# Batched gelu, a combination behind another tile, and the room of the transposed queries given to weight slots

## The chip, the cores and the metric

The kernel runs on one core of one Trainium2 chip. The metric is the time of one execution on the device in microseconds (us). A core has a matrix engine (TensorE, PE in the profile; PEld is its loading of weights), three engines for elementwise work (VectorE or DVE, ScalarE or ACT, GpSimd or POOL), and SyncE (SP), which here issues all DMA transfers. Each engine runs its own list of instructions in order and waits on semaphores for the others. TensorE writes to PSUM, eight banks per core; everything else lies in SBUF, 128 partitions wide, or in the chip's main memory.

## The reference, cut to what matters

Four residual layers over 1024 tokens of 1024 values: a mixer and a gated MLP, twice. The change lies in the first mixer alone, which projects the normalised tokens once and splits the columns: u and v (512 each) feed a gated branch, q, k and vb (512 each, eight heads of 64) feed attention in dilated windows. Both results side by side go through an output projection.

```python
u, v, q, k, vb = split(rms_norm(x, g) @ w_in)

# gated branch: chunks of 128 tokens, 8 channel groups
vn = layer_norm(gelu(v), ln_g, ln_b)
mixed = einsum('gts,bnsgc->bntgc', tril(w_s), vn) + b_s
a_out = gelu(u) * mixed

# attention: three branches, windows 128, 512, 2048, strides 1, 4, 16
qh, kh = rms_norm(heads(q), q_g), rms_norm(heads(k), k_g)
for window, dilation in ((128, 1), (512, 4), (2048, 16)):
    o, lse = dilated_branch(qh, kh, vh, window, dilation)   # softmax inside the window
b_out = sum of the branches' o, weighted by softmax of their lse

x = x + concat(a_out, b_out) @ w_out
```

Then follow the first MLP, a chunked gated linear attention, and the second MLP. All is float32 to the reader; the kernel splits an operand of a large matmul into a rounded part and a remainder (`split`, `scaled`, lines 98 to 106: the rounded part on ScalarE, the remainder on VectorE) and runs three matmuls for one product (`PASSES`).

## The kernel before

The text of the kernel is a program in one thread. A planner in the compiler lays it out when the kernel is built: it simulates the engines and writes each engine's list, where earlier text goes first among what is ready, and it adds the semaphores. `tc.keep_in_program_order(ins)` ties an instruction behind the one that the text has just before it on the same engine. A tile pool hands out room: a tag with `bufs=n` has n places in turn, and a new tile waits until the readers of the one n before it are done. Pools opened with `side="right"` lie at the other end of SBUF.

`even` (line 509) is the first mixer. The tokens come in eight tiles of 128. They are transposed and split into `hq`, and the row norms are kept in `r0`. Then come four pairs of heads (`project`, line 676, and `dilated`, line 737), the gated branch (`gmlp`, line 574; `u_proj`, line 612), and, in `out_first` (line 432), the output projection.

- `project(p)` needs eight weight pieces (`load_qkv`, line 564; tile names wq). Each is loaded raw (pool `rawp`, four places), scaled and split into one of the eight places of `wp`. The next pair's pieces, the eight of v (wv), of u (wu) and of the output projection (wo) use the same eight places one after the other. For each token tile it projects into PSUM (pj, two places), normalises queries and keys (lines 693 to 699), transposes them, and copies the queries to qT (line 713), from there to qR in the order of the strided branch (line 715, POOL), and the keys to kT. `unit` (line 650) does the attention of one token tile: scores (line 641), mask and maximum (646), exponential (647), transposes (661), product with the values (669). qT, qR and kT are as long as all tokens; pairs 0 and 2 have theirs in pool `pq0` on the right side, pairs 1 and 3 in `pq`. `par0.close()` gives the right side back behind pair 3's projection, and the gated branch's pool `gm` takes it.
- `dilated(p)` does the strided branches from qR, kT and v4 and stores the result (od). It comes back from memory as on, and `combine` and `combined` (lines 754 to 779) weigh both with an exponential (763), a few small VectorE instructions and one product on POOL and one on VectorE (776), add them (778) and store the pair's columns to `bcat` (779), one tensor per half of the tokens. For pairs 0 to 2 this runs inside the next pair's projection, behind its token tiles 3 and 4. For pair 3 it is `last` (line 804).
- `gmlp` projects v tile by tile (pv, in pj's PSUM places). `consume` (589) takes each tile through gelu, mean and variance, normalisation, gain and bias into mx; behind the last tile of each half of the tokens come eight group matmuls (pm, 605) and the additions of b_s (606).
- `u_proj` projects u (pu), takes each tile through gelu (616) and multiplies it into mx (617). Behind its fifth tile it calls `last`. The first instruction of a combination on VectorE (759) is pinned by `keep_in_program_order`.
- `out_first` loads each tile's part of bcat (cat, line 1122), transposes mx and cat (pc, 442), splits them into hq, and multiplies by wo (po, line 190 by the helper `mm_tok`).

## Time and profile before

| | us |
|---|---|
| median of 3 runs | 2196.88 (2193.66 to 2197.9) |
| the profiled execution's own time | 2195.83 |
| its span, first to last instruction | 2194.0 |
| TensorE busy | 2147.0 |
| VectorE busy | 1533.2 |
| ScalarE busy | 1042.7 |
| TensorE busy in 262 to 272 (pair 3, v) | 9.71 of 10 |
| in 272 to 332 (v, pair 3's attention) | 58.20 of 60 |
| in 332 to 394 (u) | 58.94 of 62 |
| in 394 to 405 | 1.50 of 11 |
| in 405 to 480 (output projection, first half) | 75.00 of 75 |

A line of a timeline has the start in us from the span's start, the duration, the engine, the line of the kernel, the operation, output<-inputs with the tiles' names, the shape, how many were merged, and in brackets the idle time of the engine before it with what ended it. A line of waits has who waited, for whom, the total, how many times, and the longest. A line of windows has the stretch, its length, then busy time and number of instructions of each engine, the clock granted to TensorE (1.00 is full), the share of time that the DMA engines were busy, and GB/s. A group of instructions has the line, engine, operation, tiles, shape and count, then busy us and mean ns of one, then the engine's idle time before them. An ACT_TABLE_LOAD is ScalarE exchanging its function tables, which stands under the line of the activation that needs it. Matmul ends are modelled and overlap, so a busy TensorE isn't one at its peak.

### The profile page before, as it was taken

Reading aid. Unit: us, or ns where it says so; the run is one execution under the profiler, and the core shown is the slowest. Engines: PE = TensorE matmul, PEld = TensorE weight load, DVE = VectorE, ACT = ScalarE, POOL = GpSimd, SP = SyncE. Lnnn points to the kernel's source line nnn. Section 1 sums busy time; section 2 is a strip of 40 time slices with the busy share of each in tenths; the row PEclk is TensorE's granted clock in tenths of the full one; section 3 lists DMA queues with packets and bytes.
Section 4 is the critical chain, followed back from the end, with each engine's and each line's share of the span. In section 5 each row is a group of like instructions: output and inputs, shape, how many; then the busy total and the mean of one; then the engine's idle time right before and its main releaser. Section 6 shows DMA issues by size and latency. Waiting matters only on the chain.

```text
span 2194.0 us, 29873 instructions
## 1 busy us (share of the span) xinstructions
PE 2147.0 (98%) x10508; PEld 1816.2 (83%) x10508; DVE 1533.2 (70%) x2459; ACT 1042.7 (48%) x2006; POOL 489.0 (22%) x519
## 2 busy tenths in 40 slices
PE   8999999899999999999999999999999999999999
PEld 8999987687888888878889788878788888888887
DVE  5566653567888788855577777667787878885554
ACT  6555664245444444444454455534544444454443
POOL 4444410003334342200010011110232424320000
PEclk9999999899999999999999999999999999999999
DMA  4122212565544444585563123377544454457555
GB/s 148 47 72 81 78 35 59 179 247 189 163 158 158 154 154 159 187 291 179 204 236 113 68 97 104 104 258 265 194 145 153 158 165 157 168 176 268 204 195 203
DMA packets 157254, 349.59 MB, mean 159 GB/s; under 512 B 17408, under 2 KB 54272, under 8 KB 156720
## 3 DMA queue, kind: packets, MB, share of 16 engines
q1 hardware_dynamic: 157104, 347.68, 46.9%
q8 instruction: 83, 1.36, 0.3%
q14 instruction: 67, 0.55, 0.1%
HBM read 239.02 MB, written 108.59 MB: 158 GB/s over the span
## 4 chain that ended last, share of the span: by engine, by line
PE 88%; DVE 4%; DMA 3%; ACT 3%; issue 1%; POOL 1%; SPq 0%; ACTq 0%; DVEq 0%
PE puB L290 11%; PE pgB L290 11%; PE po L190 7%; PE pj L190 6%; PE pgC L290 5%; PE puC L290 5%; PE pv L190 5%; PE pdB L397 5%; PE pdC L397 5%; PE pdO L397 4%; PE puA L290 3%; PE pgA L290 2%; PE pdP L397 2%; PE pdQ L397 2%; PE pBq L972 2%; PE pu L190 2%
## 5 line engine op out<-in xcount | busy, mean ns | idle before, releaser
L101 DVE TENSOR_TENSOR da<-ar,da 128x512 fp32r<-128x512 f32 x154 | 106.3, 690 | 156.2 <-ACT da L100 156.0
L100 ACT CAST da<-ar 128x512 fp32r<-128x512 f32 x154 | 95.9, 623 | 209.4 <-PE pdC L397 90.7
L190 PE MATMUL po<-wo,hq 128*128 128x512 f32 x768 | 186.4, 397 | 0.6 <-DVE hq L101 0.3
L190 PEld LDWEIGHTS po<-wo,hq 128*128 128x128 f32 x768 | 142.5, 189 | 30.2 <-DVE hq L101 1.4
L190 PE MATMUL pj<-wq,hq 128*128 128x384 f32 x768 | 157.8, 352 | 2.3 <-ACT vN L701 1.3
L190 PE MATMUL pv<-wv,hq 128*128 128x512 f32 (+2 forms) x768 | 141.1, 340 | 2.4 <-DVE b L1004 1.6
L190 PEld LDWEIGHTS pj<-wq,hq 128*128 128x128 f32 x768 | 135.3, 195 | 4.0 <-ACT vN L701 2.1
L397 PE MATMUL pdB<-dw,da 128*128 128x512 f32 x528 | 136.2, 391 | 0.9 <-ACT dw L100 0.9
L397 PE MATMUL pdC<-dw,da 128*128 128x512 f32 x528 | 135.8, 390 | 0.0
L190 PEld LDWEIGHTS pv<-wv,hq 128*128 128x128 f32 x768 | 118.7, 189 | 17.6 <-DVE b L1004 2.1
L397 PEld LDWEIGHTS pdB<-dw,da 128*128 128x128 f32 x528 | 98.7, 188 | 22.2 <-ACT dw L100 1.3
L397 PEld LDWEIGHTS pdC<-dw,da 128*128 128x128 f32 x528 | 99.0, 188 | 20.5
L256 POOL TENSOR_TENSOR S1g<-rg 128x512 f32<-128x512 f32 x20 | 29.3, 1464 | 384.2 <-DMA wsd<-D 325.0
L101 DVE TENSOR_TENSOR dw<-wr,dw 128x512 fp32r<-128x512 f32 x154 | 105.8, 687 | 10.7 <-ACT dw L100 10.4
L140 POOL TENSOR_SCALAR rn<-ssq 128x1 f32<-128x1 f32 x24 | 9.5, 397 | 461.3 <-ACT h L148 245.3
L397 PE MATMUL pdO<-dw,da 128*128 128x512 f32 x396 | 102.2, 389 | 0.2 <-DVE dw L101 0.2
L100 ACT CAST dw<-wr 128x512 fp32r<-128x512 f32 x154 | 95.0, 617 | 15.3 <-DMA wr<-in_w_dn 7.0
L397 PEld LDWEIGHTS pdO<-dw,da 128*128 128x128 f32 x396 | 74.3, 188 | 16.0 <-DVE dw L101 0.6
L319 DVE SCALAR_TENSOR_TENSOR t<-g,cw,t 128x1022 f32<-128x1022 f32 x44 | 75.6, 1719 | 0.1
L318 DVE SCALAR_TENSOR_TENSOR t<-g,cw,t 128x1023 f32<-128x1023 f32 x44 | 58.3, 1325 | 16.4 <-ACT t L317 16.4
L303 DVE TENSOR_TENSOR g<-g,s1g 128x512 f32<-128x512 f32 x22 | 16.2, 737 | 73.9 <-ACT s1g L302 73.9
L320 ACT ACTIVATE t<-t 128x1024 f32<-128x1024 f32 x44 | 46.7, 1061 | 29.8 <-DVE t L319 29.6
(1070 smaller groups left out, 5405.9 us busy)
## 6 DMA issues: line engine op xcount, KB each, us to landing
ar<-actd SPq DMA_DIRECT2D x70, 512.0 KB, 3.5
rd<-in_w_down SPq DMA_DIRECT2D x44, 512.0 KB, 3.6
wsd<-D SPq DMA_DIRECT2D x88, 256.0 KB, 2.6
rg<-in_w_gate SPq DMA_DIRECT2D x42, 512.0 KB, 3.6
ru<-in_w_up SPq DMA_DIRECT2D x42, 512.0 KB, 4.6
wr<-wsd SPq DMA_DIRECT2D x40, 512.0 KB, 4.5
actd<-t SPq DMA_DIRECT2D x66, 256.0 KB, 2.1
wr<-in_w_dn SPq DMA_DIRECT2D x30, 512.0 KB, 5.0
```

What stands on the lines that cost most here:

```text
L100: (hi or A.copy)(dst[0], src)
L101: (lo or V.tensor_sub)(dst[1], src, f32(dst[0]))
L140: G.tensor_scalar(r, ssq, 1.0 / n, EPS, op0=ALU.mult, op1=ALU.add)
L190: T.matmul(o, L[i], R[jj][:, sl], start=(k == 0 and (ii, jj) == PASSES[0]), stop=(k == nk - 1 and (ii, jj) == PASSES[-1]))
L256: G.tensor_tensor(sums[name], x, y, op=op)
L290: T.matmul(o, L[ii][:, j * P : j * P + P], right[p][:, jj, j, :], skip_group_check=more, start=(not more and j == 0 and (ii, jj) == PASSES ...
L303: V.tensor_add(C22, C22, s1)
L318: V.scalar_tensor_tensor(t[:, 1:], g[:, : S - 1], w(1), t[:, 1:], op0=ALU.mult, op1=ALU.add)
L319: V.scalar_tensor_tensor(t[:, 2:], g[:, : S - 2], w(0), t[:, 2:], op0=ALU.mult, op1=ALU.add)
L320: A.activation(t, t, AF.Silu)
L397: T.matmul(o, L[ii][:, t * P : t * P + P], R[jj], skip_group_check=more, start=start and not more and (ii, jj) == PASSES[0], stop=stop and ...
L972: T.matmul(o, L[ii][:, j * P : j * P + P], right[p][:, jj, j, :], skip_group_check=more, start=(not more and j == 0 and (ii, jj) == PASSES ...
```

## The change

Four things in `even`'s functions, none in what is computed.

- v's tiles are scaled by their row norm while they are copied from PSUM to mx. Behind the fourth tile of a half one gelu runs over all four (128x2048, in place), then the four normalisations and the group matmuls. The second half's gelu is pinned behind the copy before it. The tag gv goes, and u's tiles get their own tag ut with five places in place of gv's two.
- `last` is called behind u's second tile in place of its fifth.
- qT is a tile of one token tile (128x2x128), with three places in `pq` for all pairs, in place of one tile for all tokens in `pq0` and one in `pq`.
- A pool `wx` on the right side, opened ahead of `pq0` and closed with it, has four places of 128x2x384. The first four of the eight weight pieces of pairs 0 and 2 are split into it; the other four, and all of pairs 1 and 3, go to `wp` as before.

```diff
+            wx = par0.enter_context(tc.tile_pool(name="wx", bufs=4, side="right", reuse_waits="tile"))
             pq0 = par0.enter_context(tc.tile_pool(name="pq0", bufs=1, side="right", reuse_waits="tile"))
...
-    def load_qkv(p):
-        return [w for kp in range(4)
-                for w in load_w(a["w_qkv"][p, kp], f"wq{p}{kp}", 384, gains=g0[:, 2 * kp : 2 * kp + 2])]
+    def load_qkv(p, wx):
+        ws = []
+        for kp in range(4):
+            raw = load_raw(a["w_qkv"][p, kp], f"wq{p}{kp}r", 768)
+            for i in range(2):
+                k = 2 * kp + i
+                src, gain = raw[:, i * 384 : i * 384 + 384], g0[:, k : k + 1]
+                if p % 2 or k >= 4:
+                    ws.append(parts_of(src, f"wq{p}{kp}_{i}", gain=gain))
+                else:
+                    w = wx.tile([P, 2, 384], F32R, tag="wx", name=f"wx{p}{k}")
+                    ws.append([w[:, j, :] for j in range(2)])
+                    scaled(ws[-1], src, gain)
+        return ws
...
         def consume(n, pj):
-            gv = gm.tile([P, 512], F32, tag="gv", bufs=2, name=f"gv{n}")
-            A.activation(gv, pj, AF.Gelu, scale=r0[:, n : n + 1])
...
-            r = inv_rms(mv[:, 1:2], 1, 1, f"lr{n}")
-            V.tensor_scalar(gv, gv, mv[:, 0:1], r, op0=ALU.subtract, op1=ALU.mult)
-            V.tensor_mul(gv, gv, lnG)
             half, j = n // 4, n % 4
-            V.tensor_add(mx[half][:, j, :], gv, lnB)
-            if j == 3:
-                for g in range(GROUPS):
...
+            A.activation(mx[half][:, j, :], pj, AF.Copy, scale=r0[:, n : n + 1])
+            if j < 3:
+                return
+            ge = A.activation(flat(mx[half]), flat(mx[half]), AF.Gelu)
+            if half:
+                tc.keep_in_program_order(ge)
+            for j in range(4):
+                gv = mx[half][:, j, :]
...
+                r = inv_rms(mv[:, 1:2], 1, 1, f"lr{half}{j}")
+                V.tensor_scalar(gv, gv, mv[:, 0:1], r, op0=ALU.subtract, op1=ALU.mult)
+                V.tensor_mul(gv, gv, lnG)
+                V.tensor_add(gv, gv, lnB)
+            for g in range(GROUPS):
...
         def consume(n, pj):
-            t = gm.tile([P, 512], F32, tag="gv", bufs=2, name=f"ut{n}")
+            t = gm.tile([P, 512], F32, tag="ut", bufs=5, name=f"ut{n}")
             A.activation(t, pj, AF.Gelu, scale=r0[:, n : n + 1])
             V.tensor_mul(mixed[n], mixed[n], t)
-            if n == 4:
+            if n == 1:
                 last()
...
             pool = pq if p % 2 else pq0
-            qT = pool.tile([P, 2, S], F32R, tag="qT", bufs=1, name=f"qT{p}")
             qR = pool.tile([P, 2, S], F32R, tag="qR", bufs=1, name=f"qR{p}")
...
-                A.copy(qT[:, :, ts_], f32(tq))
+                qT = pq.tile([P, 2, P], F32R, tag="qT", bufs=3, name=f"qT{p}{n}")
+                A.copy(qT, f32(tq))
...
-                G.tensor_copy(four(qR), by4(f32(qT[:, :, ts_])))
+                G.tensor_copy(four(qR), by4(f32(qT)))
...
-                unit(p, f"{p}n{n}", n % 4, ot, po, lambda s: qT[:, s, ts_],
+                unit(p, f"{p}n{n}", n % 4, ot, po, lambda s, qT=qT: qT[:, s],
```

More of the change, by code (lines that the diff above doesn't have):

```diff
@@ L538, in even @@
                     tc.tile_pool(name="av", bufs=1, reuse_waits="tile") as av:
-                return attention(ps, at, av, pq, pq0, par0, wq0, masks, gm_open)
+                return attention(ps, at, av, pq, pq0, par0, wx, wq0, masks, gm_open)
     def band_masks(pool):
@@ L589, in consume @@
         def consume(n, pj):
[L590 to L606 removed]
+            half, j = n // 4, n % 4
+            A.activation(mx[half][:, j, :], pj, AF.Copy, scale=r0[:, n : n + 1])
[6 more added lines that the diff above has]
+                gv = mx[half][:, j, :]
+                st = small.tile([P, 6], F32, tag="bn", name=f"bn{half}{j}")
+                V.bn_stats(st, gv)
+                mv = small.tile([P, 2], F32, tag="mv", name=f"mv{half}{j}")
+                V.bn_aggr(mv, st)
+                r = inv_rms(mv[:, 1:2], 1, 1, f"lr{half}{j}")
[3 more added lines that the diff above has]
+            for g in range(GROUPS):
+                gc = mx[half][:, :, g * 64 : g * 64 + 64]
+                pm = ps.tile([P, 4, 64], F32, tag="sc", name=f"pm{half}{g}")
+                T.matmul(pm, ws[:, g, :], gc, start=True, stop=True)
+                V.tensor_scalar(gc, pm, bs[:, g : g + 1], None, op0=ALU.add)
         mx = [gm.tile([P, 4, 512], F32, name=f"mx{h}") for h in range(2)]
@@ L614, in consume, with attention @@
         def consume(n, pj):
[L615 removed]
+            t = gm.tile([P, 512], F32, tag="ut", bufs=5, name=f"ut{n}")
             A.activation(t, pj, AF.Gelu, scale=r0[:, n : n + 1])
             V.tensor_mul(mixed[n], mixed[n], t)
[L618 removed]
+            if n == 1:
                 last()
         proj512(ps, load_half(a["w_vu"][1], "wu", g0), "pu", consume)
[L623 removed]
+    def attention(ps, at, av, pq, pq0, par0, wx, wq0, masks, gm_open):
         gqk = pq.tile([P, 2, 2, 64], F32, name="gqk", bufs=1)
```

13 lines of the change are left out of this document (2 added, 11 removed).

## The prediction

> **What bounds the kernel now.** I read the page first (span, busy shares), then TensorE's waits in the first 420 us, where all changed code runs, then ten-microsecond windows with the granted clock, and last the order of time on each engine around the largest wait. All times below are those of the one profiled execution.
>
> ```profile
> span 2194.0 us, 29873 instructions
> PE 2147.0 (98%) x10508; PEld 1816.2 (83%) x10508; DVE 1533.2 (70%) x2459; ACT 1042.7 (48%) x2006; POOL 489.0 (22%) x519
> ```
>
> TensorE is busy for 98% of the span, so a change that removes none of its matmuls can only gain where it waits or where its clock is reduced.
>
> ```profile
> PE pc L442 <- DMA cat<-bcat: 9.3, 1, 9.3
> PE pP3d L661 <- ACT sm3d L647: 3.3, 3, 2.0
> PE po0n L669 <- DVE pT0n L666: 2.2, 2, 1.9
> PE pP1n L661 <- ACT sm1n L647: 1.4, 2, 1.0
> PE pj L190 <- ACT vN L701: 1.3, 3, 0.6
> PE pu L190 <- ACT ut L616: 0.9, 1, 0.9
> ```
>
> One wait is nearly three times the next: the transposes of the output projection (pc, line 442) stand 9.3 us for a load of bcat, the attention's combined heads. The next, 3.3 us, is a transpose that waits for the last pair's exponentials.
>
> ```profile
> core 0: us, PE busy (x) PEld busy (x) DVE busy (x) ACT busy (x) POOL busy (x), PEclk, DMA share, GB/s
> 60.00:70.00 10.00, 8.10 (x52) 7.87 (x51) 9.44 (x21) 6.14 (x15) 5.54 (x8) 0.92 0.39 107
> 70.00:80.00 10.00, 9.62 (x60) 9.41 (x59) 4.36 (x14) 4.85 (x14) 5.96 (x11) 0.91 0.22 68
> 140.00:150.00 10.00, 8.37 (x37) 7.70 (x38) 4.98 (x15) 4.51 (x14) 6.55 (x11) 0.68 0.32 102
> 330.00:340.00 10.00, 7.96 (x45) 6.90 (x44) 8.69 (x22) 9.94 (x20) 0.74 (x2) 0.91 0.60 184
> 360.00:370.00 10.00, 8.98 (x39) 6.76 (x38) 4.47 (x9) 1.29 (x2) 0.00 (x0) 1.00 0.34 83
> 403.40:406.00 2.60, 2.34 (x7) 1.60 (x8) 1.25 (x2) 1.07 (x2) 0.00 (x0) 0.50 1.03 387
> 406.00:409.00 3.00, 3.00 (x12) 2.60 (x12) 0.74 (x2) 0.59 (x1) 0.00 (x0) 0.50 1.00 405
> 409.00:412.00 3.00, 3.00 (x12) 2.40 (x12) 0.69 (x1) 0.59 (x1) 0.00 (x0) 0.87 0.44 125
> ```
>
> The column after POOL is the granted clock. It is 0.50 after the long wait, and 0.92, 0.91, 0.68 and 0.91 in the windows at 60, 70, 140 and 330 us, where TensorE also stood.
>
> ```profile
> 362.39 1.52 SPq L788 DMA_DIRECT2D on<-od  x2
> 367.42 1.29 DVE L617 TENSOR_TENSOR mx<-mx,ut 128x512 f32<-128x512 f32 x2
> 385.92 0.69 DVE L617 TENSOR_TENSOR mx<-mx,ut 128x512 f32<-128x512 f32 x1
> 386.53 0.16 DVE L759 TENSOR_TENSOR cM<-ot3n,on 128x8 f32<-128x8 f32 x1
> 393.23 0.36 SPq L779 DMA_DIRECT2D bcat<-ot3n  x1
> 397.82 0.47 SPq L1122 DMA_DIRECT2D cat<-bcat  x1
> 384.94 8.78 PE L190 MATMUL pu<-wu,hq 128*128 128x512 f32 x37
> 393.56 0.60 PE L442 MATMUL pc<-ident,mx 128*128 128x128 f32 x4
> 403.41 1.12 PE L442 MATMUL pc<-ident,cat 128*128 128x128 f32 x4 [9.25 <-DMA cat<-bcat]
> 404.77 1.22 PE L190 MATMUL po<-wo,hq 128*128 128x512 f32 x2 [0.25 <-ACT hq L100]
> ```
>
> This is why that load is late. The other operands of the last combination (on) were asked for at 362.39, but its first VectorE instruction (line 759) runs at 386.53, right behind the product of u's fifth tile (line 617, 385.92): program order pins it there, and that product needs the second half of the gated values. So the first half's store to bcat leaves at 393.23, the load that reads it at 397.82, and TensorE, through with u at 393.7, goes on at 403.41.
>
> **The change, part by part.**
>
> *Last combination behind u's second tile.* It removes and adds no instruction; twenty VectorE instructions, two exponentials, two products on POOL (idle in the row at 360) and two stores on SP move, the stores ahead of the loads of wo's second half. The new pin is the product of tile 1, which needs only the first half of the gated values. Both products of tiles 0 and 1 already ran from 367.42 on, and on was asked for at 362.39, so the combination can start near 368. Its load can follow 11.3 us later (386.53 to 397.82 now), near 380, and land after another 5.6 (397.82 to 403.41), near 386, against 394 when it is wanted: 8 us of cover. What is removed: the 9.25 us. What is late next: the output projection's weights. The last rounding of wo on ScalarE and its remainder on VectorE are these:
>
> ```profile
> 394.68 0.61 ACT L100 CAST wo<-wo03r 128x512 fp32r<-128x512 f32 x1
> 398.55 0.68 DVE L101 TENSOR_TENSOR wo<-wo03r,wo 128x512 fp32r<-128x512 f32 x1
> ```
>
> VectorE reaches the last remainder only at 398.55 because the combination's instructions from 386.53 on lie between the remainders. Without them it follows ScalarE's 394.68 + 0.61 and ends near 396.0. TensorE starts the first tile at 393.56 + 0.60 + 1.36 = 395.5 (the first transposes, then 403.41 to 404.77 as now) and needs this eighth piece last. So none of this wait stays; with VectorE as late as now (399.2) it would be at most 3.7 us. The clock: by the three rows from 403.40, 2.6 x 0.50 + 3.0 x 0.50 + 3.0 x 0.13 = 3.2 us were withheld, part of it while TensorE waited for hq (before 404.77); I take 2.5. The Trainium skill ("TensorE: Matmul & The Clock Gate", Part 1: The HAM clock gate) has half the clock after an idle window of about 3.4 us and until about 3.4 us of sustained work; by that the term would be 1.7 instead of 2.5, an estimate, and the sum 0.8 us smaller. The trace agrees on the half and shows it for at least 5.6 us.
>
> At its new place the combination shares VectorE (4.47 of 10 us busy at 360) and ScalarE (1.29) with little. Behind its first instruction, if on lands late, wait the additions of the second half's gated values (line 606) and, through their PSUM tiles, TensorE. on was asked for 5 us ahead of the products now; I charge 1.25 us for this and for two table loads between gelus, with 0 and 2.6 as bounds (two loads of the size below). Together: -9.25 - 2.5 + 1.25 = -10.5. Bounds: -9.25 - 3.2 = -12.5, and -9.25 + 3.7 + 2.6 = -3.0 if wo and the two loads are paid and the clock gives nothing.
>
> *Batched gelu.* Now each of v's eight tiles has its own gelu among the last pair's exponentials, and ScalarE exchanges its tables for each:
>
> ```profile
> L647 ACT ACT_TABLE_LOAD x9 | 11.5, 1283 | 12.1 <-DVE ot3d L646 6.5 <-DVE ot3n L646 5.5
> L591 ACT ACT_TABLE_LOAD x8 | 10.3, 1283 | 0.1
> L616 ACT ACT_TABLE_LOAD x3 | 3.8, 1283 | 0.3 <-PE pu L190 0.3
> 382.67 1.28 ACT L763 ACT_TABLE_LOAD   x1
> L148 ACT ACTIVATE n<-xt 128x1024 f32<-128x1024 f32 x8 | 8.6, 1074 | 16.9 <-DVE xt L429 15.8 <-ACT n L148 0.7 <-issue 0.5
> ```
>
> That is 21 loads of 1.283 us, 27 us. Two batches need two exchanges each, the combination two, u's first tiles some two: about 8, so 13 x 1.283 = 16.7 us go from ScalarE. Eight copies take the place of eight gelus on the same tiles, at about the same price; the two gelus of 128x2048 come on top, at twice the 1.07 us of the 128x1024 row, 4.3 in all. ScalarE gains 12 us, but it bounds nothing here: on TensorE only the waits behind it count, 3.3 + 0.9 of those quoted, and the clock at 330 (10 x 0.09 = 0.9), 5.1 together. Against it: one batch holds up every exponential behind it for 1.28 + 2.15 + 1.28 = 4.7 us, where now each gelu holds them up for half of that. TensorE has v's next tile to run meanwhile, since the copies empty its two PSUM tiles ahead of the gelu. VectorE gets a half's normalisation (four tiles of some 3 us) in one run, but it lies behind the attention in program order. ut gets five buffers in place of two, so the 0.9 us wait for ut goes. I take half: -2.5, with -5.1 and +4.7 (one batch uncovered) as bounds. The pin on the second batch names the copy just before it, on which it depends anyway; I give it nothing.
>
> *Four weight slots for even pairs.* Today the eight pieces of a pair are all split at the turn to the next pair, as slots come free:
>
> ```profile
> 60.00:70.00 10.00, 6.11 (x30) 5.45 (x29) 5.51 (x8) 4.44 (x8) 0.92 0.39 107
> 130.00:140.00 10.00, 8.07 (x44) 7.06 (x43) 6.12 (x8) 4.47 (x8) 1.00 0.48 126
> ```
>
> VectorE spends 5.51 and 6.12 of ten microseconds on them (the third busy time of a row, here of these splits alone), just where TensorE waits for pT0n (2.2 us) and sm1n (1.4). With the change pair 0 leaves four of the common slots free for pair 1, and pair 2 finds its own four free since pair 0; half of each burst, about 2.9 us of VectorE and 2.2 of ScalarE, moves ahead of the turn into windows where both have room. It adds no work; each split and its matmuls are as before. What is behind the bursts on TensorE: the waits 2.2 + 1.4 + 1.3, and the clock, 0.8 + 0.9 at 60 and 70 and 3.2 at 140: 9.8 us. The combinations stay at the turn, and four splits too, so I take two fifths: -4.0, with -9.8 as one bound. The other is +3: half a burst set in front of a row of exponentials elsewhere.
>
> *Queries per token tile.* Same copies (line 713) and readers; three tiles of room in place of eight. A tile's scores must be through before the copy three tiles on:
>
> ```profile
> 272.36 0.36 ACT L713 CAST qT<-tq 128x256 fp32r<-128x256 f32 x1
> 287.26 0.37 ACT L713 CAST qT<-tq 128x256 fp32r<-128x256 f32 x1
> 277.88 0.64 PE L641 MATMUL sc3n<-kT,qT 128*128 128x256 f32 x4
> 298.70 0.72 PE L641 MATMUL sc3n<-kT,qT 128*128 128x256 f32 x4
> ```
>
> In the last pair a copy's scores follow 5.5 us (272.36 to 277.88) to 11.4 us (287.26 to 298.70) behind it, and two copies further on lie 14.9 us: a ring of three isn't full. Zero, with 0 and the rival below as bounds.
>
> Sum: -10.5 - 2.5 - 4.0 + 0 = -17.0. The profiled execution took 2195.83 us (1.83 around its span of 2194.0) and the median of the three runs is 2196.88, 1.05 more. So 2195.83 - 17.0 + 1.05 = 2179.9; I say 2180. All that lies behind moves up with it, since TensorE is busy for 98% of the span.
>
> **Rivals.**
>
> *The ring of three becomes the wait: slower.* If each of the 32 tiles' copies waits for scores, ScalarE stands, and behind it exponentials and the emptying of pj. It decides from 17.0 / 32 = 0.53 us per tile; at 0.8 us the time is 2197 - 17 + 26 = 2206. For it: the planner's new order isn't known, and scores of a tile come up to 11.4 us late. Against: 14.9 us between copies.
>
> *Batches hold up the attention.* Both batches uncovered cost 9.4 us in place of the gain of 2.5: 2180 + 11.9 = 2192, or 2187 to 2189 with one and some of the weights' gain lost as well. For it: the wait for sm3d is of this kind already.
>
> *The load stays late or another takes its place.* If SP or VectorE puts the combination behind other work again, the largest term fails and 2197 - 6.5 = 2190 is left. Against: its pin, and 8 us of cover.
>
> *Nothing moves.* The batch loses what the slots gain, and the cat wait turns into one for wo and the DMA engines, which are busy to 1.03 and 1.00 at 403 and 406: 2197.
>
> *The clock doesn't come back.* Behind u TensorE has only transposes and a short wait. If transposes don't hold the clock, the output projection starts at 0.50 as now: 2180 + 2.5 = 2182.5. In the trace 140 us is such a stretch, mostly attention, at 0.68. The Trainium skill ("TensorE: Matmul & The Clock Gate", Part 4: PE-mode transpose) says that a transpose doesn't count as busy for the gate; the low clock at 140 agrees, but other waits stand there too. The stretch is about 2 us, so I give it little.
>
> **How the numbers follow.** Forecast 0.45; clock 0.12; batches 0.17; load late 0.10; nothing moves 0.05; slower 0.11. Faster by over 0.2% (4.4 us, about what a measurement of this kernel can tell from no change): 0.84; same 0.05; slower 0.11. The range runs from 2170, where the slots give 9.8 and the gelu 5.1 with some new wait against them, to 2193, which takes in the batches and the late load; what is left out is nothing moved, slower, and a little below: 0.2. The forecast's own range is 2172 to 2186.
>
> **What would show it.** Right: no wait of pc for cat; the combination's line 759 on u's pair near or before 370; clock near 1.00 right behind u; table loads in the first 420 us of about 8 in place of 21; fewer splits of wq in the windows of the turns, and waits there under 3 us. Wrong: a new wait of over 3 us at pP3d or pm behind the 128x2048 gelu, waits of ScalarE in front of qT, or the projection po waiting for wo.

## The result and the profile after

The changed kernel takes 2184.73 us (median of five runs, 2180.52 to 2186.67); the kernel before, on the same chip, 2197.45 (2193.66 to 2201.47). The ratio is 0.9943, with a 95% interval of 0.9925 to 0.9961: 12.7 us faster, where 17.0 were forecast. The profiled execution took 2186.67, 1.7 around its span. On the page:

```profile
span 2185.0 us, 29867 instructions
PE 2145.9 (98%) x10508; PEld 1817.9 (83%) x10508; DVE 1538.2 (70%) x2459; ACT 1032.7 (47%) x1998; POOL 488.4 (22%) x519
```

TensorE's busy time hardly moved (2147.0 to 2145.9); what went is waiting. From its list of waits in the first 420 us (waiter, whom for, total, times, longest):

```profile
PE pt L530 <- DMA x<-in_x: 5.5, 2, 4.4
PE tk L736 <- ACT qT L731: 1.7, 3, 0.6
PE pc L442 <- DVE hq L101: 1.7, 1, 1.7
```

The 9.3 for cat and the 3.3 for sm3d are gone. What is late next is small: pc for hq, 1.7, and the queries' copy, 1.7 in three parts. The timelines of VectorE, SyncE and TensorE show the combination in its new place:

```profile
366.30 1.29 DVE L635 TENSOR_TENSOR mx<-mx,ut 128x512 f32<-128x512 f32 x2
367.51 0.16 DVE L777 TENSOR_TENSOR cM<-ot3n,on 128x8 f32<-128x8 f32 x1
374.69 0.96 SPq L797 DMA_DIRECT2D bcat<-ot3n  x2
377.04 0.33 SPq L1140 DMA_DIRECT2D cat<-bcat  x1
387.08 0.44 PE L442 MATMUL pc<-ident,mx 128*128 128x128 f32 x2 [0.67 <-DVE mx L624]
387.36 0.38 PE L442 MATMUL pc<-ident,cat 128*128 128x128 f32 x2
388.41 0.73 PE L190 MATMUL po<-wo,hq 128*128 128x512 f32 x2 [0.24 <-ACT hq L100]
```

It starts right behind the first products, at 367.51 (386.53 before), its load leaves at 377.04 (397.82 before), and TensorE transposes cat at 387.36 with no wait. ScalarE's table loads and the batched gelu, in the groups of the stretch from 262 to 420:

```profile
L665 ACT ACT_TABLE_LOAD x4 | 5.1, 1283 | 0.1
L634 ACT ACT_TABLE_LOAD x4 | 5.1, 1283 | 0.1
L607 ACT ACTIVATE mx<-mx 128x2048 f32<-128x2048 f32 x2 | 3.8, 1918 | 0.0
L607 ACT ACT_TABLE_LOAD x2 | 2.6, 1283 | 0.0
L781 ACT ACT_TABLE_LOAD x1 | 1.3, 1283 | 0.0
```

Eleven loads in place of 21 (I had said about 8: u's tiles still fall among the last exponentials, with four loads).

**Where the time went.** The span is cut at TensorE's first or last matmul on a tile, read from its timeline: the end of pair 0's values (po0n), the start and end of v (pv), the end of u (pu), the first po, the first matmul of the MLP (pgB), the end of the span. Durations in us, of one profiled execution each; the experiments of the next section stand below the line of the changed kernel.

| kernel | to po0n's end | to v | v | u | to po | output proj. | rest |
|---|---|---|---|---|---|---|---|
| before | 91.14 | 180.76 | 59.98 | 61.84 | 11.05 | 102.28 | 1686.95 |
| changed | 95.80 | 176.84 | 55.21 | 58.13 | 2.43 | 106.16 | 1690.43 |
| changed, again | 95.92 | 176.83 | 55.18 | 58.13 | 2.43 | 106.09 | 1686.82 |
| 1: combination | 91.98 | 177.42 | 59.97 | 60.77 | 1.77 | 101.52 | 1689.87 |
| 2: gelu | 90.79 | 177.22 | 55.16 | 60.18 | 11.09 | 101.52 | 1689.14 |
| 3: slots and ring | 93.68 | 178.03 | 60.02 | 62.17 | 12.18 | 104.61 | 1690.61 |
| 3, again | 98.50 | 176.80 | 60.05 | 61.96 | 11.53 | 103.25 | 1690.61 |
| 4: changed, two places for u | 92.28 | 176.93 | 55.18 | 60.20 | 1.78 | 101.50 | 1691.03 |
| 5: gelu + combination | 90.69 | 180.39 | 55.17 | 60.21 | 1.77 | 100.28 | 1687.59 |
| 5, again | 91.61 | 178.96 | 55.17 | 60.21 | 1.77 | 100.28 | 1686.90 |
| 6: slots for pair 2 | 92.09 | 176.98 | 55.17 | 60.21 | 1.77 | 101.55 | 1690.83 |
| 7: 5 + 6 KB unused | 89.83 | 177.42 | 55.17 | 60.20 | 1.78 | 106.24 | 1687.16 |
| 8: 5 + five places, other room | 92.22 | 180.35 | 55.17 | 58.13 | 2.44 | 102.40 | 1689.29 |
| 9: ring | 92.14 | 179.12 | 61.13 | 60.75 | 10.99 | 103.54 | 1688.53 |

The changed kernel gains 4.8 in v, 3.7 in u and 8.6 ahead of po, and 3.9 up to v, but loses 4.7 in pair 0 and 3.9 in the output projection. In the rest, where no text was changed, two executions of one kernel differ by 3.6 (1690.43 and 1686.82; 1.7 of it is a stretch at half clock at 1445 us that only the first has), so nothing is read from that column, nor from a difference of 3 us between two spans.

The first two columns differ mostly by the clock. Take off the time that it withheld ahead of v (half the length of each stretch at half clock: 5.1 us before and in both executions of the changed kernel, 0 to 8.5 in the others). Then v's first matmul comes at 266.1 to 267.7 us in the eight executions without the four weight slots, and at 266.8 to 268.3 in the six with them. Up to there the slots neither gain nor lose anything that can be told apart from the clock.

Two things in the changed kernel weren't forecast. The first is a wait in the second half of the output projection (line 497 loads the first half of a row tile xt from xd, line 498 the second from the input, line 430 stores xh to xd, line 429 adds po):

```profile
444.78 0.42 SPq L430 DMA_DIRECT2D xd<-xh  x1
450.76 0.33 SPq L497 DMA_DIRECT2D xt<-xd  x1
455.33 0.69 DVE L429 TENSOR_TENSOR xt<-xt,po 128x512 f32<-128x512 f32 x1 [9.61 <-DMA xt<-in_x]
```

SyncE stands from 445.75 + 0.33 to 450.76 ahead of the first load of xt, and VectorE waits 9.61 us for the load behind it. SyncE's own list of waits from 438 to 453 says what for, the landing of that last store of xh, which is of another row tile; TensorE's, from 420 to 520, shows what reaches it:

```profile
SPq L497 <- DMA xd<-xh: 4.6, 1, 4.6
PE pt L162 <- DVE xt L152: 2.3, 1, 2.3
```

The second is that two of the three bursts of weight splits at the turns weren't halved. The windows of line 106 alone (the first busy time is VectorE's, with the number of splits), before and after:

```profile
0.00:40.00 40.00, 4.49 (x8) 1.00 0.58 193
60.00:80.00 20.00, 5.51 (x8) 0.91 0.31 88
130.00:150.00 20.00, 6.12 (x8) 0.84 0.40 114
196.00:220.00 24.00, 5.12 (x8) 1.00 0.34 111
```

```profile
0.00:40.00 40.00, 6.79 (x12) 1.00 0.62 212
60.00:80.00 20.00, 5.20 (x8) 0.83 0.28 86
130.00:150.00 20.00, 5.21 (x8) 1.00 0.37 113
196.00:220.00 24.00, 3.19 (x4) 1.00 0.25 77
```

Eight at the first two turns stay eight, and four more come in the start-up; the third turn, from pair 2 to pair 3, has four in place of eight. There was little to gain at that one: TensorE's waits from 196 to 225 are 0.8 us before and 1.0 after, with the clock at 1.00 in both. And the clock, the figure behind POOL's instructions in a window's row:

```profile
40.00:50.00 10.00, 8.47 (x60) 7.91 (x60) 8.02 (x23) 7.31 (x22) 5.11 (x10) 0.83 0.01 2
70.00:80.00 10.00, 9.63 (x43) 8.78 (x42) 4.50 (x12) 2.59 (x8) 3.22 (x6) 0.69 0.25 83
140.00:150.00 10.00, 8.90 (x62) 7.70 (x61) 8.12 (x21) 5.29 (x16) 7.17 (x12) 1.00 0.49 155
300.00:340.00 40.00, 40.00 (x218) 34.29 (x217) 26.35 (x73) 29.94 (x54) 8.04 (x16) 1.00 0.18 57
380.00:390.00 10.00, 8.24 (x39) 6.14 (x37) 9.42 (x16) 6.62 (x11) 0.00 (x0) 1.00 0.96 327
390.00:400.00 10.00, 9.18 (x49) 7.72 (x50) 4.80 (x8) 2.34 (x4) 0.00 (x0) 1.00 0.37 124
```

It is 1.00 behind u, as forecast, and 1.00 at 140, where it was 0.68; but 0.83 and 0.69 at 40 and 70.

### The profile page after: what moved, and what is told of

Its sections match the earlier page's. It is cut to its first block, busy times and chain, and to the rows that moved or that the text cites. A ratio compares the mean times of both kernels' runs of the same rounds, so it can differ in the third digit from the quotient of the medians.

```text
span 2185.0 us, 29867 instructions
## 1 busy us (share of the span) xinstructions
PE 2145.9 (98%) x10508; PEld 1817.9 (83%) x10508; DVE 1538.2 (70%) x2459; ACT 1032.7 (47%) x1998; POOL 488.4 (22%) x519
## 4 chain that ended last, share of the span: by engine, by line
PE 70%; DMA 4%; DVE 3%; ACT 1%; issue 1%; SPq 0%; POOL 0%; DVEq 0%; ACTq 0%
PE puB L290 11%; PE pgB L290 11%; PE pgC L290 5%; PE puC L290 5%; PE pdB L397 5%; PE pdC L397 5%; PE pv L190 4%; PE pdO L397 4%; PE puA L290 3%; PE pgA L290 3%; PE po L190 2%; PE pdQ L397 2%; PE pdP L397 2%; PE pBq L990 2%; PE pBr L990 2%
## 5 line engine op out<-in xcount | busy, mean ns | idle before, releaser
L190 PE MATMUL pj<-wq,hq 128*128 128x384 f32 x576 | 118.1, 348 | 0.0
L101 DVE TENSOR_TENSOR dw<-wr,dw 128x512 fp32r<-128x512 f32 x154 | 105.9, 687 | 11.2 <-ACT dw L100 11.1
L190 PEld LDWEIGHTS pj<-wq,hq 128*128 128x128 f32 x576 | 101.0, 192 | 0.4 <-ACT vN L718 0.2
L397 PEld LDWEIGHTS pdO<-dw,da 128*128 128x128 f32 x396 | 74.3, 188 | 15.9 <-DVE dw L101 0.6
L303 DVE TENSOR_TENSOR g<-g,s1g 128x512 f32<-128x512 f32 x22 | 16.2, 738 | 77.1 <-ACT s1g L302 77.1
```

Of the source, the lines that this page charges most:

```text
L101: (lo or V.tensor_sub)(dst[1], src, f32(dst[0]))
L190: T.matmul(o, L[i], R[jj][:, sl], start=(k == 0 and (ii, jj) == PASSES[0]), stop=(k == nk - 1 and (ii, jj) == PASSES[-1]))
L303: V.tensor_add(C22, C22, s1)
L397: T.matmul(o, L[ii][:, t * P : t * P + P], R[jj], skip_group_check=more, start=start and not more and (ii, jj) == PASSES[0], stop=stop and ...
```

## The experiments

Theories. *Mine after the result:* the combination is worth about what was forecast, the gelu more, the slots nothing or less, since the planner refills freed places at once, and the 6 KB of u's three added places move the output projection's tiles so that xt lies where xh lay. *Rivals:* the slots gain and something hides it; the late xt comes of starting earlier, not of places; the ring costs. All times below are medians, with the ratio to the kernel before on the same chip.

**1. The combination alone.**

```diff
-            if n == 4:
+            if n == 1:
                 last()
```

> The kernel before with one edit: the last combination behind u's second tile in place of its fifth. Theory (the order of VectorE alone made cat late): pc waits for cat no longer, the first po starts about 10 us earlier than the 404.77 of before, near 394 to 395, with the clock near 1.00 there; the second half of the output projection keeps the memory places it has before, so its xt loads meet no late store, the wait of xt for in_x stays under 2 us, and the start of the first MLP moves by the same 9 to 10: about 2188. Rival A (the new xt wait in the second half of the output projection comes of starting earlier, with the loads and stores of the hidden stall now in the open): the same gain at po, then 4 us given back ahead of the first MLP: about 2192. Rival B (the combination needs the lighter ScalarE of the batched gelu): cat's wait shrinks to 3 to 5 us only: about 2192, with a wait of pc left.

Measured: 2187.93 against 2195.45, ratio 0.9962 (0.9949 to 0.9976). TensorE behind u, and the clock in the window at 140:

```profile
389.98 0.38 PE L442 MATMUL pc<-ident,mx 128*128 128x128 f32 x2
390.19 0.38 PE L442 MATMUL pc<-ident,cat 128*128 128x128 f32 x2
391.91 0.73 PE L190 MATMUL po<-wo,hq 128*128 128x512 f32 x2 [0.90 <-ACT hq L100]
```

```profile
140.00:150.00 10.00, 8.34 (x57) 7.43 (x56) 5.59 (x17) 4.67 (x14) 7.14 (x12) 1.00 0.41 121
```

The wait for cat is gone without any help from the gelu, so rival B falls. From v's end on 9.28 + 1.07 + 0.76 = 11.1 us are saved, and nothing is given back in the output projection (101.52), so rival A falls too. The clock is 1.00 in the windows from 130 to 510. That at 140 matters: the text ahead of it is that of the kernel before, which had 0.68 there.

**2. The batched gelu alone**, u's tiles with two places.

```diff
-            A.activation(gv, pj, AF.Gelu, scale=r0[:, n : n + 1])
...
+            A.activation(mx[half][:, j, :], pj, AF.Copy, scale=r0[:, n : n + 1])
+            if j < 3:
+                return
+            ge = A.activation(flat(mx[half]), flat(mx[half]), AF.Gelu)
```

> The kernel before with one edit: v's gelu in two batches of 128x2048; u's tiles have two places as before, so that the room is the same. The prediction's term was -2.5. In the comparison of before and after v's end moved by 4.0 and u's end by 7.7 with 0.7 lost ahead of v, so the theory is that the batches alone bring v's end forward by 4 to 5 us (near 327), u's end by 5 to 7; the cat wait stays at 8 to 10 since the combination hangs on u's fifth tile: about 2191 to 2192. Rival (u's gain came from the moved combination or from u's five places): u's end moves by no more than 4 to 5 and the time is 2193 or more. Rival from the prediction (batches hold up the attention): a new wait of 3 us or more at pP3d or pm, 2197 or above.

Measured: 2188.84 against 2195.45, ratio 0.9971 (0.9957 to 0.9985). v is 4.8 us shorter, u 1.7, the same to 0.1 us wherever the batches appear with two places (2, 4, 5, 6, 7 in the table). TensorE's wait for sm3d isn't in its list any more, and the one for ut is 0.6 in place of 0.9; the one for cat is as before:

```profile
PE pc L442 <- DMA cat<-bcat: 9.3, 1, 9.3
```

By these stretches the batches are worth 6.5, not 2.5, and no wait behind them is seen. Of that, 1.1 need not be theirs: the kernel before lost 1.7 us of clock at 338 to 342, experiments 1 and 9 lost none there in these executions, and their u takes 60.77 and 60.75 with no batch at all.

**3. The slots and the ring alone**, twice.

```diff
+            wx = par0.enter_context(tc.tile_pool(name="wx", bufs=4, side="right", reuse_waits="tile"))
...
+                if p % 2 or k >= 4:
...
+                qT = pq.tile([P, 2, P], F32R, tag="qT", bufs=3, name=f"qT{p}{n}")
```

> The kernel before with two edits that belong together: the four weight slots on the right side and the transposed queries per token tile. The prediction's term was -4.0. Theory after the comparison (the freed common slots are filled at once with pair 1's first pieces, in the start-up, so the burst moves by one pair and isn't halved): as many splits of wq at each turn as before (8), pair 0's last po near 95 to 96 in place of 91.1, v's first matmul within 1 us of 271.9, time 2197 to 2199. Rival (the slots gain and something else in the change hid it): v's first matmul at 268 or earlier, time 2193 or less.

Measured: 2199.35 against 2195.45, ratio 1.0019 (1.0008 to 1.0029).

> The kernel of the slots and the ring alone, a second time, for its places that move from profile to profile. If its loss (3.9 us against the kernel before) is of the kernel: again 1.001 to 1.003 of it, a cat wait of 10 or more, 104 to 105 us from the first po to the first MLP, and no dip of the clock at 130 to 150. If it was chance: within 0.1% of the kernel before, 9.3 and 102.

Measured the second time: 2203.54 against 2195.18, ratio 1.0038 (1.0025 to 1.0052). This part makes the kernel slower, by 3.9 and 8.4 us, in place of the forecast gain of 4.0. Pair 0 ends at 93.68 and 98.50 in place of 91.14. Most of the second number is clock:

```profile
40.00:50.00 10.00, 8.47 (x53) 7.90 (x52) 8.01 (x23) 6.92 (x21) 5.10 (x10) 0.74 0.01 2
70.00:80.00 10.00, 8.60 (x35) 8.30 (x36) 5.68 (x12) 1.55 (x5) 4.55 (x9) 0.66 0.47 144
```

With 0.26 and 0.34 of ten microseconds withheld here (and 2.5 more at 50, 0.75), TensorE lost 8.5 us of full clock. The stretch to v, by contrast, is 176.8 to 178.0 with the slots, where the kernels without them show 177.2 to 180.8; that too is mostly the clock at 140, without which the ranges are 176.3 to 177.0 and 175.7 to 177.4. So v begins at 271.71 and 275.30, against 271.90 before, and with the withheld clock taken off at 268.3, 266.8 and 266.8: the start-up shows little of the loss. Behind v, up to the first MLP, the two executions take 3.8 and 1.6 us more than the kernel before, with the same 8.5 us withheld. All runs together say the same: by their spans and granted clocks the kernel before had 10.3 us withheld on the one chip and 11.2 on the other, this one 11.7 and 15.4, and with that taken off it is 3.5 and 3.7 us slower (an estimate, since the clock of a run is given to 0.001, 2.2 us of it): about that much of the loss is not clock. The wait for cat was 10.4 and then 9.7, the output projection 104.61 and 103.25: both above the kernel before, not as large the second time; I have no cause for that part.

**4. The changed kernel with two places for u's tiles.**

```diff
-            t = gm.tile([P, 512], F32, tag="ut", bufs=5, name=f"ut{n}")
+            t = gm.tile([P, 512], F32, tag="ut", bufs=2, name=f"ut{n}")
```

> The changed kernel with two places for u's tiles in place of five, which makes the gated branch's pool 6 KB smaller and puts the output projection's tiles where the kernel before has them. Theory (in the changed kernel the xt tiles of the first MLP's input lie where xh lay, and so wait for xh's last store): the xt wait for in_x at 450 to 465, 9.6 us on VectorE, goes below 2, TensorE's wait for xt there goes with the 0.83 clock; 4.4 us come back and the wait for ut takes up to 1: about 2181, the first MLP's first matmul near 490 to 491 in place of 494.6. Rival (the wait is due to the loads and stores of the earlier start, not to places): it stays at 8 to 10 and the time is 2185 to 2186.

Measured: 2182.49 against 2195.45, ratio 0.9943 (0.9928 to 0.9957). SyncE's queue:

```profile
441.70 0.45 SPq L430 DMA_DIRECT2D xd<-xh  x1
443.25 0.50 SPq L497 DMA_DIRECT2D xt<-xd  x1
```

The first load of xt leaves 1.55 us behind the last store of xh, not 5.98 as in the changed kernel, and the output projection takes 101.50 in place of 106.16. One half of the expectation failed: VectorE still waits 8.3 us for xt, but ends that wait in time for TensorE, which waits 0.7. u takes 2.1 more (60.20). By the traces the five places save 2.07 in u and cost 0.65 in the stretch to po and 4.66 in the output projection: 3.2 lost. By the ratios it is 0 to 2 us (0.9943 and 0.9951 for the changed kernel), which their intervals can't tell from 3.

**5. Gelu and combination without slots and ring**, twice, the second time on one chip with the changed kernel. The edits of experiments 1 and 2 together.

> The kernel before with batched gelu (two places for u's tiles) and the combination behind u's second tile, without the weight slots and the queries' ring. Theory (the slots only cost): the start-up is that of before, with pair 0's first po near 44 to 45 in place of 47 to 48, v begins near 268 to 269, and the gains of the two edits alone add up, 7.5 + 6.6: about 2181 or a little less, 1 to 4 below the same kernel with slots (2182.5). Rival (the slots are neutral once the gelus are batched): the same time as with slots, 2182 to 2184.

Measured: 2178.18 against 2194.35, ratio 0.9933 (0.9921 to 0.9945).

> Batched gelu with two places and the moved combination, without slots and ring, a second time, beside the changed kernel. Theory: 3 to 6 us below the changed kernel, of which 4 to 5 stand between the first po and the first MLP (100 to 101.5 us in place of 105 to 106); the dip of the clock at 130 to 150 may be there or not. If the difference were of the chips and not of the kernels: within 2 us of it.

Measured: 2179.26 against 2195.18, ratio 0.9929 (0.9917 to 0.9942).

> The changed kernel a second time, on the same chip as the next one. Theory: 0.994 of the kernel before; the first xt load again 6 us or more behind the last store of xh, 105 to 106 us from the first po to the first MLP; the clock between 40 and 80 need not dip as in its first profile, whose 95.8 for pair 0's last po then falls to 91 to 93.

Measured for the changed kernel beside it: 2183.77, ratio 0.9951 (0.9939 to 0.9964). So the kernel with two of the four parts is 4.5 us faster than the changed one (all its runs, 2177.02 to 2180.8, lie below all of the other's, 2181.0 to 2186.22), and with that of experiment 6, from which it isn't told apart, the fastest of all that ran. The output projection takes 100.28 both times, 106.09 in the changed kernel. The expectation of fewer dips in the changed kernel failed: it had 0.83 at 40 and 0.68 at 70 again. The two executions of the other kernel differ from each other in the clock at 140, 0.66 and 0.83 (below).

**6. The added slots for pair 2 alone**, u with two places.

```diff
-                if p % 2 or k >= 4:
+                if p != 2 or k >= 4:
```

> The changed kernel with two places for u's tiles, and the four extra weight slots used by pair 2 alone; pair 0 takes all eight common slots again. Theory (what the slots cost is the start-up, where the common slots left free by pair 0 let pair 1's first pieces be scaled and split ahead of pair 0's own work): no split of pair 1 before 40 us, pair 0's first po back at 44 to 45, and v's first matmul no later than without slots, 268 to 269; the turn from pair 1 to pair 2 has four splits fewer, which may bring up to 1.5 (the wait for pair 1's exponentials there): 2179 to 2182. Rival (the queries' ring of three is what costs): the waits of tk for qT stay at 1.7 and the first po at 46 to 48, 2183 or above.

Measured: 2178.45 against 2194.35, ratio 0.9932 (0.992 to 0.9944): the same as without slots. The splits of line 106:

```profile
0.00:40.00 40.00, 4.48 (x8) 0.96 0.57 193
60.00:80.00 20.00, 7.79 (x12) 1.00 0.44 129
130.00:150.00 20.00, 5.13 (x8) 1.00 0.41 119
196.00:220.00 24.00, 3.19 (x4) 1.00 0.26 76
```

Pair 2's four went to the turn before, twelve now, and at the turn to pair 2 there are eight again and not four as expected, since the common places that pair 2 leaves free take pair 3's pieces at once; the four fewer are at the last turn. A freed place is filled at the next moment that frees a raw place, and that moment is always a turn or the start-up. The time is that of experiment 5, but this doesn't show that the start-up is where the slots cost: pair 0's first po starts at 46.72, not at 44 to 45 as expected (46.84 in experiment 4, with all slots), pair 0 ends at 92.09 with 1.7 us of clock withheld at 20 to 30 (0.83), v begins at 269.07 where experiment 4 has 269.21, and the interval holds experiment 4's ratio.

**7. Gelu and combination with an unused tile of 6 KB** in the gated branch's pool.

```diff
+        gm.tile([P, 1536], F32, name="pad6")
         lnG = gm.tile([P, 512], F32, name="lnG")
```

> The kernel before with batched gelu and the moved combination, and an unused tile of 6 KB in the gated branch's pool, which does nothing but shift the output projection's tiles to where the changed kernel has them. Theory (places alone make the late xt): the first xt load leaves SyncE about 6 us behind the last store of xh (1.6 in the kernels with the smaller pool), and from the first po to the first MLP pass 105 to 106 us in place of 101.5: 4 to 5 us above the same kernel without the tile. Rival (the five places of u's tiles or the slots did it): 1.6 us, 101.5, and the same time.

Measured: 2183.3 against 2194.35, ratio 0.9949 (0.9936 to 0.9962), by the medians 5.1 us above the same kernel without the tile on the same chip; the two intervals overlap, and the means of the runs differ by 3.6. SyncE's queue, then SyncE's waits from 438 to 453 and TensorE's from 420 to 520:

```profile
438.71 0.37 SPq L430 DMA_DIRECT2D xd<-xh  x1
446.41 0.33 SPq L497 DMA_DIRECT2D xt<-xd  x1
```

```profile
SPq L497 <- DMA xd<-xh: 6.1, 1, 6.1
PE pt L162 <- DVE xt L152: 4.5, 2, 4.1
```

The load leaves 7.7 us behind the store; 106.24 in place of 100.28. The tile holds nothing: places alone make this wait, which again ends with the store's landing. That xt then lies just where xh lay is the likeliest reading; no trace shows addresses.

**8. Five places for u, with other room for xt.** Meant to keep u's gain without its price: the MLP's temporaries get their room first, so that the first xt lies over vectors and the first half of the gated values.

```diff
+        for tag, cols, bufs in (("t", S, 4), ("S", 512, 4), ("u", 2 * S, 1)):
+            pool.tile([P, cols], F32, tag=tag, bufs=bufs, name=f"room{l}{tag}")
         mine = {}
```

> Meant to beat both kernels: the kernel before with batched gelu, the moved combination and five places for u's tiles, and the temporaries of the MLP's input given their room ahead of the xt tiles, so that the first xt lies where the gated branch's vectors and first half lay, which are read earlier than xh is stored. Theory: u passes 2 us faster than with two places (58 in place of 60), the first xt load no longer waits for the last store of xh, VectorE's wait of 7 to 9.6 us for it shrinks to 3 or less, from the first po to the first MLP pass 100 to 101.5 us: 2 to 3 below the same without these two, about 2178. Rival (the xt wait is hidden from TensorE anyway when the load leaves 1.6 us behind the store, and the places of u's tiles are worth nothing): within 1 us of it.

Measured: 2180.94 against 2194.35, ratio 0.9939 (0.9926 to 0.9951). The expectation failed in the sum: it isn't below experiment 5. The load leaves 1.4 us behind the store again (444.95 and 446.32), and the output projection takes 102.40, not 106.1; but SyncE's list has the load behind that store anyway, so it can't leave earlier, and VectorE waits 7.6 as without the edit. u's 2.1 are there; 0.7 goes in the stretch to po and 2.1 in the output projection against experiment 5.

**9. The queries' ring alone.**

```diff
-            qT = pool.tile([P, 2, S], F32R, tag="qT", bufs=1, name=f"qT{p}")
...
+                qT = pq.tile([P, 2, P], F32R, tag="qT", bufs=3, name=f"qT{p}{n}")
```

> The kernel before with one edit: the transposed queries kept per token tile, three places, without the weight slots. The prediction had 0 for this. Theory: no new wait of ScalarE ahead of the queries' copy, no wait of tk for qT beyond 1, v's first matmul at 267 to 269 where TensorE's clock holds and at 271 to 272 where it dips near 140, 2193 to 2197. Rival (the ring is what made the kernel with slots slower): waits of tk for qT of 1.7 as with the slots and 2 or more above the kernel before.

Measured: 2197.04 against 2195.18, ratio 1.001 (0.9998 to 1.0022): no difference that can be told, and one wait for qT in TensorE's list, 0.55 at 211.8. The kernels with slots for pairs 0 and 2 have three (1.7), experiment 6 has two (1.1), those without the ring none: a third of it comes with the ring alone, the rest with ring and slots together.

## Why the prediction was right, and where it was not

Sign and range (faster, 2170 to 2193) held; the sum, 4 us off, came near by luck: one term too small and one of the wrong sign nearly cancelled.

- *Combination, -10.5:* right. Alone it measured -11.1 from v's end to the MLP (1.07 of it in u, where the clock from 340 to 380 is 1.00 in place of 0.98, which need not come of the move), -7.5 by the medians (-11.2 to -5.3 by the interval). The gap behind u went from 11.05 to 1.77; its start (368 forecast, 367.51), its load (380, 377.04) and the 8 us of cover came as worked out, though of other parts: the load landed 2.7 us behind its issue, not 5.6, at 379.7, and was wanted at 387.4, 7.7 us later, since u ended earlier too. wo's last remainder lies at 389.47 in the changed kernel, ahead of its use. I had charged 1.25 for the new place; no wait there is seen.
- *Clock behind u, -2.5 inside that term:* right in sign; the windows from 380 on show 1.00. The output projection of experiment 1 is only 0.76 shorter, since a wait of 0.9 for hq stands at its start, so no more than 1.7 of it is seen. The Trainium skill ("TensorE: Matmul & The Clock Gate", Part 1: The HAM clock gate) halves the clock only after an idle window of about 3.4 us; the two waits left here are 0.67 and 1.67 us long and the clock stays at 1.00, which agrees; the last section has a lull with less waiting that did cost clock, so that it stays was not sure. The rival on transposes isn't decided by this: the stretch with nothing else is 1.3 us (387.08 to 388.41).
- *Batched gelu, -2.5:* the mechanism right, the size wrong; it measured -6.5 (-6.6 by the medians, -9.4 to -3.3 by the interval). I listed 5.1 of waits and clock behind the table loads and took half for fear of 4.7 us of hold-up. The cover that I named myself, v's next tile in the emptied PSUM places, was enough: TensorE is busy 40.00 of 40 from 300 to 340. Of the other 1.4, 0.8 is the rest of the same dip of the clock, of which I had read one row alone (0.91 at 330; the next, at 340, has 0.92); what is left isn't named by any row. That dip is the 1.7 which experiments 1 and 9 lack without a batch. The batch is also cheaper than the row that I scaled: 1.92 us, not 2.15.
- *Four weight slots, -4.0:* wrong. The step that failed is "half of each burst moves ahead of the turn into windows where both have room". The splits in the start-up and at the three turns went from 8, 8, 8, 8 to 12, 8, 8, 4: a place set free is refilled when its raw tile lands, and the text and the planner put that into the start-up and the turns. Only the last turn was halved, and it had nothing to give (0.8 us of waits before, 1.0 after). Alone the term is +3.9 and +8.4, beyond the bound of +3, but not by what stood behind that bound ("half a burst set in front of a row of exponentials elsewhere"): up to v little but the clock differs, and the 3.8 and 1.6 us behind v have no cause on record. Inside the whole it is some +2 (experiment 4 against 5: 0.9943 and 0.9933), which the intervals don't tell from nothing.
- *The clock of the turns, 4.9 of the 9.8 on which that term rests:* I took the 0.68 at 140 for a property of the bursts. Experiment 1 has 1.00 there with the same text and the same eight splits; experiment 5 has 0.66 and 0.83 in two executions. It comes and goes with the same code (the last section shows how); it was seen at 140 in no execution of the six with slots in `wx`, whose waits from 130 to 150 add up to 1.2 to 1.3 us in place of 1.6 to 2.5, and in five of the eight without. That much of the forecast gain is there: of the eight splits at that turn only four are of the pair that starts. At the other end TensorE's waits from 36 to 50 are 1.5 in the changed kernel, 1.2 before, and in both its executions the clock falls there instead.
- *Queries per tile, 0:* right (1.001, 0.9998 to 1.0022). The rival "ring of three" didn't come.
- *u's five places:* I credited 0.9 for the wait and priced the room at nothing. u got 2.1 shorter, and the 6 KB cost 4.7 in the output projection. The sentence that failed is "all that lies behind moves up with it": 16.4 us of gain reached the first po (404.77 to 388.41), 12.5 the MLP (507.05 to 494.57). The profile before showed the tiles but not their addresses; the diff showed that the pool grows.

Added up by the experiments: gelu and combination together -16.2 and -15.9, the slots +2.2 (0.9943 less 0.9933, of 2195), five places 0 to +1.8: -14.0 to -11.9, against -12.7 and -11.4 measured. This is no check, since each term is the difference between one of these kernels and the next. The two parts together bring a little more than apart (7.5 + 6.6 = 14.1), within the intervals.

What isn't settled: where the slots alone lose the some 3.5 us that are not clock; whether the clock falls at 40 in the kernels with slots because of those longer waits (all five with pair 1's pieces in the start-up lost clock between 20 and 60; of the nine others one, experiment 6, did), and why the output projection takes 103 to 105 us in those with slots or ring but tile-wise gelu.

## What to carry to other kernels

Read a long wait back to the instruction that stands last in an engine's list for no reason of data, as line 759 did here: that term came out nearly to the microsecond, and the table exchanges between two users of one engine were worth here the whole wait behind them on the bound engine, which had other work meanwhile. More places for a prefetch need not flatten a burst if what frees them comes at the same moments as before (here two turns of three kept their eight splits, and the one that was halved had cost nothing): count the loads per window, and ask when the next refill happens. A reduced clock in one profile may not be there in the next execution of the same code: look at a second one before a gain is forecast from it. A pool's size is part of a change: a tile that grows by a few KB can push a later tile onto room that is still being stored, so price what starts behind it.

## What the runs showed of the hardware that was not expected

- A lull of TensorE costs its clock in one execution and not in the next. Experiments 1 and 5 have the same matmuls between 139 and 146 (two transposes of queries, four of probabilities, four of keys, eight products 64 wide) with the same waits between them (0.98, 0.41 and 0.26; 0.96, 0.41 and 0.26). Windows of 2 us, experiment 5 first, then experiment 1:

```profile
140.00:142.00 2.00, 0.78 (x4) 0.42 (x5) 1.45 (x6) 1.71 (x6) 1.21 (x3) 1.00 0.69 198
142.00:144.00 2.00, 1.74 (x11) 1.60 (x11) 0.79 (x2) 1.07 (x2) 1.85 (x5) 0.71 0.01 4
144.00:146.00 2.00, 2.00 (x11) 2.00 (x11) 0.71 (x3) 0.44 (x2) 0.80 (x1) 0.50 0.11 33
148.00:150.00 2.00, 2.00 (x8) 2.00 (x8) 0.45 (x1) 0.00 (x0) 0.40 (x2) 0.59 0.38 113
```

```profile
140.00:142.00 2.00, 1.16 (x8) 0.78 (x6) 2.00 (x8) 0.52 (x3) 1.69 (x2) 1.00 0.96 268
142.00:144.00 2.00, 1.29 (x8) 0.80 (x8) 1.16 (x4) 1.73 (x7) 1.36 (x3) 1.00 0.51 175
144.00:146.00 2.00, 1.90 (x16) 1.90 (x17) 0.86 (x3) 1.01 (x4) 1.93 (x3) 1.00 0.00 0
```

  The first has half the clock from 143 to 149, 3.4 us withheld in some 6.8; the second none; the second execution of experiment 5's kernel 1.7 us in some 3.5 (0.57 and 0.58 in the windows at 144 and 146). The Trainium skill ("TensorE: Matmul & The Clock Gate", Part 1: The HAM clock gate) says that activity is judged in free-running windows of 3413 ns, so that the moment of a change depends on where in a window the work falls; the half clock, the lengths of one and two such windows and the difference between executions agree with that. Each trace shows its own grid: inside the span of each of the 14, all changes of the clock lie whole multiples of 3.413 us apart (338.11, 341.52, 396.13 and 409.78 in the kernel before), and the windows can be counted from them. In experiment 5 one runs from 139.41 to 142.83; TensorE is busy for 1.79 of its 3.42 us, transposes included, and the clock falls at its end. In experiment 1 the same lull lies across 139.87 to 143.28 and 143.28 to 146.70, with 2.02 and 3.16 busy, and the clock stays. Where the same part asks for an idle window of that length, the trace differs: 1.6 us of waits among transposes and narrow products were enough. Ahead of each of the 32 falls between 10 and 500 us in the 14 traces TensorE was busy for 0.70 of the window or less, though windows down to 0.45 kept the clock.
- A tile of 6 KB that no instruction touches made the kernel 5.1 us slower by the medians (3.6 by the means), through a load that could leave only 7.7 us behind a store in place of 1.6.
- One gelu over 128x2048 took 1918 ns, where a copy of 128x512 (line 604 of the changed kernel) takes 681: four tiles in one instruction cost less than three apart.
